# Hybrid mLSTM and sparse-attention block on one core: the output product in two passes, keys ahead of queries, masks on GpSimd

## The chip, the core and the metric

The kernel runs on one core of one Trainium2 chip. The metric is the device time of one execution in microseconds (us). The engines are TensorE (PE in the profile), VectorE (DVE), ScalarE (ACT), GpSimd (POOL) and the queues that issue DMAs, of which SyncE's (SP) issues nearly all loads. Each engine works through its own instructions in the order in which the program gives them.

## The reference, cut to what matters

512 tokens of width 1024, in float32. One combined projection feeds two head groups, whose results go through one output product.

```python
u = rmsnorm(h, norm_in[i])
proj = u @ w_in[i]                      # 1024 -> 6736 columns, split into 13 parts
...
hm = mlstm_chunkwise(mq, mk, m_v, log_i, log_f)          # 4 heads, 1024 features
hm = sigmoid(m_o) * (hm * rsqrt(mean(hm * hm)) * m_norm) * silu(m_z)
ha = dsa_attention(a_q, a_k, a_v, ix_q, ix_k, ix_w, rel_bias)   # 8 heads of 64, top 128 keys
ha = ha * silu(a_z)                                      # 512 features
h = h + concatenate([hm, ha], axis=-1) @ w_out[i]        # 1536 -> 1024
h = h + (p[i] @ w_ple[i]) * sigmoid(h @ w_ple_gate[i])
return rmsnorm(h, norm_final)
```

In the attention, logits of keys that the indexer did not select are masked, and a bias by distance is added.

## The kernel before, in words

**Products.** Every float32 operand of a product is kept as two parts, a rounded one (H) and the rest (L), and a product is three matmuls (H·H, H·L, L·H) of 128x128 weights over 512 columns. One such triple is a *step* of a dense generator: `dense_fm` (features on partitions) or `dense_tm` (tokens on partitions). Each ends with an evacuation of its PSUM bank. Dense products rotate over four PSUM banks (`mm_bank`), everything else over four others (`x_bank`).

**Weights.** `plan` lists the weight slabs in the order of use. SP loads a slab into `raw` (three buffers), ScalarE makes `wh`, VectorE or, for every second slab from 40 to 60, GpSimd makes `wl` (line 161, `work`). One job of this kind is issued per step.

**Order.** PE, VectorE, ScalarE and GpSimd are ordered by hand: `tick()` runs after each step; `later(n, f)` issues `f` after n ticks; `back` holds generators that are advanced by a credit. `weave(main, fill, rate)` gives `rate` steps of dense work to each unit of the main generator.

**Stages.** Input norm and the indexer's queries; mLSTM features; from about 240 us on the woven stages. `weave(mlstm(), ...)` takes 3.5 dense steps a unit, and its dense work ends with `attention_in(0)` (queries and keys of head pair 0, two banks `aqk`) and the attention's values (`av`, four banks). `weave(attention(), ...)` then has 32 units, (head, block of 128 queries), and 5 more to drain: `logits` (line 793) multiplies, `least` (line 803, VectorE) adds the mask and takes the smallest, ScalarE exponentiates, `norm` scales, `flip` (line 829, `pt_ps`) transposes on PE, `values` multiplies with the values, `close` gates a head pair and splits it into mixH/mixL 8 to 11. `masks` (lines 785 to 791) prepares mask plus bias of the next unit one tick after a unit: `sel[i]` plus the bias `tz`, the far part on GpSimd, the near 256 columns on VectorE. Its dense work: pairs 1 to 3 (16 steps each), `az` (the gate, four banks, 32 steps), and the first 40 of 48 steps of `project(0)`, the output product's left 512 columns over all 12 feature tiles (0 to 7 from the mLSTM, 8 to 11 from the attention). Then its last 8 steps, `project(1)` with 48, the transposes of h, the product with p, the gate product and the last norm.

`evac_aqk` (line 764) is what empties the two `aqk` banks of a pair: bank b=0 are the queries, b=1 the keys. The query part needs two ScalarE and two VectorE instructions, the key part four and four. Between the ends of the two banks lie 4 steps, because a slab of a pair holds 4 feature tiles:

```python
if b == 0:    # queries: ScalarE at ticks 0, 1; VectorE at ticks 2, 3
else:         # keys: ScalarE at ticks 0 to 3; VectorE at ticks 4 to 7
```

`evac_out` (line 887) adds the residual, which was loaded as `xr` (1 MB each) into the buffer of the bias `tz`. At the end of the program token block 3 is done in two halves (`evac_last`, line 1013), while block 2 goes through `evac_gate1` (line 1006).

Of the kernel before, what the change touches and what calls it, by code (L numbers as in the profile page):

```python
# [13 lines left out]
F32 = mybir.dt.float32  # L14
# [18 lines left out]
NTMP, NHM, NKEEP = 7, 3, 37  # L33
COST_SC, COST_CV, COST_TK, COST_MX, RATE_M, RATE_A = 1.2, 1.6, 2.0, 2.0, 3.5, 3.2
SPLITP = range(40, 62, 2)
# [13 lines left out]
def block_kernel(ctx: ExitStack, tc: tile.TileContext, x, p, w_in, b_gate, conv_w, w_out, norm_in,  # L49
# [36 lines left out]
    def f(ap):  # L86
        return ap.bitcast(F32)
# [42 lines left out]
    def slab(src, k0, nk, cols):  # L130
        plan.append(([src[k0 * P:(k0 + nk) * P, c:c + m] for c, m in cols], nk))
# [76 lines left out]
    def pair(b):  # L208
        return [(C_AQ + P * b, P), (C_AK + P * b, P)]

    for cols in ([(C_IQ, S)], [(C_MQ, S)], [(C_MK, S)], [(C_MV, S)], [(C_MV + S, S)], [(C_MO, S)], [(C_MZ, S)],
                 [(C_MO + S, S)], [(C_MZ + S, S)], pair(0), [(C_AV, S)], pair(1), pair(2), pair(3), [(C_AZ, S)]):
        nk = KP * S // sum(m for _, m in cols)
        for k0 in range(0, KT, nk):
            slab(w_in[0], k0, nk, cols)
    for c in range(2):
        for k0 in range(0, 12, KP):
            slab(w_out[0], k0, KP, [(c * S, S)])
    for c in range(2):
# [544 lines left out]
    def evac_aqk(pair):  # L764
        def go(b, ps):
            half = [slice(0, 64), slice(64, 128)]
            for s in range(2):
                h, me, other = 2 * pair + s, half[s], half[1 - s]
                if b == 0:
                    t = aq[h] = keep(f"aq{h}", F32R)  # L770
                    later(s, A.activation, t[me, :], ps[me, :], AF.Copy, 0.0, -DH ** -0.5)
                    later(s + 2, V.scalar_tensor_tensor, t[other, :], ps[me, :], -DH ** -0.5, f(t[me, :]),
                          OP.mult, OP.subtract)
                else:
                    t1, t2 = ak1[h], ak2[h] = keep(f"ak1_{h}", F32R), keep(f"ak2_{h}", F32R)
                    for q, o in enumerate((me, other)):
                        later(2 * s + q, A.activation, t1[o, :], ps[me, :], AF.Copy)
                        later(2 * s + q + 4, V.tensor_tensor, t2[o, :], ps[me, :], f(t1[me, :]), OP.subtract)
        return go

    def attention():
# [3 lines left out]
        def masks(h, i):  # L785
            n = (i + 1) * P
            t = prob[h, i] = tmp("pr", shape=(P, n))
            if i > 1:
                G.tensor_scalar(t[:, 0:n - 256], sel[i][:, 0:n - 256], tz[:, h, 0:1], None, op0=OP.add)
            if i > 0:  # L790
                V.tensor_tensor(t[:, n - 256:], sel[i][:, n - 256:], tz[:, h, :], OP.add)

# [71 lines left out]
        for k in range(NT * AH + 5):  # L864
            if k < n:
                logits(*units[k])
            if k + 1 < n:
                later(1, masks, *units[k + 1])
            if k in values_at:
                h = values_at[k]  # L870
                values(h)
                if h % 2:
                    later(4 if h > 3 else 48 if h == 1 else 24, close, h // 2)
            if k in turns_at:
                flip(*turns_at[k])
            yield
# [4 lines left out]

    hs, xr = {}, {}

    def evac_out(c):
        def ev(i, ps):
            t = hs[i, c] = keep(f"h{i}_{c}")
            V.tensor_tensor(t, ps, xr[c][:, i, :], OP.add)
            if c:
                later(2, turn_h, c, i, mm_bank("hT_ps").rearrange("p (k t) -> p k t", t=P))
        return ev  # L890

    def project(c):
        yield from dense_tm(lambda kt, i: mixH[kt][:, i * P:(i + 1) * P], lambda kt, i: mixL[kt][:, i * P:(i + 1) * P],
                            list(range(12)), evac_out(c), name="wo", late=c == 0)

    def load_residual(c):
        t = xr[c] = sp.tile([P, NT, S], F32, tag="tz", bufs=1, name=f"xr{c}")
        nc.sync.dma_start(t, x[0, :, c * S:(c + 1) * S].rearrange("(i p) c -> p i c", p=P))

# [14 lines left out]
    while not ended[0]:  # L914
        tick()
    pace[0] = 1.0
    out0 = project(0)
    weave(attention(), chain(attention_in(1), attention_in(2), attention_in(3), dense_fm(4, evac_az, name="az"),
                             (next(out0) for _ in range(40))), lambda k: RATE_A)
    load_residual(0)  # L920
    plt = sp.tile([P, SW], F32, tag="sH", bufs=1, name="plt")
    pl = plt[:, 0:NT * DPLE].rearrange("p (i c) -> p i c", c=DPLE)
    nc.sync.dma_start(pl, p[0, 0].rearrange("(i p) c -> p i c", p=P))
    run(out0)

# [12 lines left out]
    def turns():  # L938
        for i in range(NT):
            turn_h(0, i, x_bank("hT_ps", (P, 4, P)))  # L940
            yield 4.0
        for k in range(2):
# [5 lines left out]
            later(2, V.tensor_tensor, pL[k], ps, f(pH[k]), OP.subtract)  # L948
            yield 4.0

# [12 lines left out]

    load_residual(1)
    back.append(turns())
    run(project(1))


# [36 lines left out]

    def evac_gate1(i, ps):
        sg = soft(i, 1, ps, 0, S)
        later(1, add, sg, i, 1, 0, S)
        later(3, square, sg, i, 1, 0, S, fs[i][:, 1:2])
        later(4, factor, i)  # L1010
        later(6, store, i)

# [53 lines left out]
    for kt in range(KT):  # L1066
        gate_step(2, ps, slice(0, S), kt)
    evac_gate1(2, ps)
    parts = [mm_bank(f"wg3_{q}") for q in range(2)]
# [44 lines left out]
```

## Time and profile before

| what | value |
|---|---|
| median of 3 runs | 527.8 us (526.2 to 528.93) |
| the profiled execution's own time | 527.67 us |
| its span, first to last instruction | 525.1 us |
| mean granted clock of PE | 0.986 of full speed |
| ScalarE, share of the span busy | 50% |
| HBM read / written | 48.13 MB / 3.69 MB |

Times in the trace are counted from the start of the span. "Idle before, releaser" names what ended an engine's idle time. Because the matmuls' ends are modelled and overlap, the distance from one matmul's start to the next is what a matmul costs; a clean step of three is 0.70 us.

### The profile page before, as it was taken

To read this page: it belongs to the slowest core of one execution; us is meant where nothing else is said; L and a number is where in the kernel's file an instruction comes from. 1 tells how busy PE (TensorE), PEld (TensorE's weight loads), DVE (VectorE), ACT (ScalarE), POOL (GpSimd) and SP (SyncE) were. 2 spreads that over 40 slices of the span, in tenths; PEclk is the share of its full clock that TensorE was granted. 3 is DMA by queue.
4 is the path that set the end of the run, shared out by engine and by line. 5 is a ranking of instruction groups with operands and counts; after the bars stand their busy time and mean duration, and the time that the engine had idled before them with its cause. 6 is when DMAs were issued, how large, how long until landed. Compare 5 with 4: busy or idle time off the path is not lost.

```text
span 525.1 us, 6781 instructions
## 1 busy us (share of the span) xinstructions
PE 500.9 (95%) x2370; PEld 410.3 (78%) x2370; DVE 353.8 (67%) x766; ACT 265.1 (50%) x574; POOL 77.4 (15%) x118
## 2 busy tenths in 40 slices
PE   5899999999999999999979999879999999999994
PEld 4887888888788878888768888668888888778783
DVE  1944577878899599878872787785795343350944
ACT  6643676543425135654743686775775334140542
POOL 4400000000010002020221333223332110000000
PEclk9999999999999999999979999999999999999998
DMA  8442564223543133331322222121214444050213
GB/s 267 129 157 53 69 126 116 88 93 103 167 149 104 57 97 114 97 118 54 112 59 80 62 60 81 40 81 41 81 51 151 163 158 160 24 172 5 81 40 119
DMA packets 37280, 52.24 MB, mean 99 GB/s; under 512 B 4156, under 2 KB 16732, under 8 KB 37248
## 3 DMA queue, kind: packets, MB, share of 16 engines
q1 hardware_dynamic: 32192, 45.49, 27.1%
q10 hardware_dynamic: 4960, 6.31, 5.6%
q8 instruction: 18, 0.29, 0.2%
q14 instruction: 14, 0.11, 0.1%
q0 software_dynamic: 96, 0.02, 0.0%
HBM read 48.13 MB, written 3.69 MB: 99 GB/s over the span
## 4 chain that ended last, share of the span: by engine, by line
PE 76%; DVE 12%; ACT 5%; issue 3%; DMA 1%; POOL 1%; SPq 0%; POOLq 0%; ACTq 0%; DVEq 0%
PE wo L258 4%; PE wo L260 4%; PE wo L259 4%; PE mv L260 3%; PE mv L259 3%; PE mv L258 3%; PE o L238 2%; PE o L236 2%; PE o L237 2%; PE z L236 2%; PE z L238 2%; PE z L237 2%; DVE wl L161 2%; DVE ak L194 2%; PE mq L236 1%
## 5 line engine op out<-in xcount | busy, mean ns | idle before, releaser
L161 ACT ACTIVATE wh<-raw 128x512 fp32r<-128x512 f32 x140 | 83.4, 623 | 14.7 <-DMA raw<-in_w_ple_gate_dram 5.7
L161 DVE TENSOR_TENSOR wl<-raw,wh 128x512 fp32r<-128x512 f32 x118 | 78.6, 684 | 5.1 <-ACT wh L161 4.9
L161 POOL TENSOR_TENSOR wl<-raw,wh 128x512 fp32r<-128x512 f32 x22 | 29.2, 1336 | 91.2 <-issue 57.2
L258 PE MATMUL wo<-wh,mixH 128*128 128x512 f32 x96 | 39.3, 410 | 0.0
L260 PE MATMUL wo<-wh,mixL 128*128 128x512 f32 x96 | 37.8, 394 | 0.0
L259 PE MATMUL wo<-wl,mixH 128*128 128x512 f32 x96 | 37.8, 394 | 0.0
L811 ACT ACTIVATE pr<-pr,sm 128x128 f32<-128x128 f32 (+3 forms) x32 | 17.9, 560 | 17.0 <-DVE sm L803 16.8
L569 DVE MAX8 m<-sc 128x8 f32<-128x256 f32 (+2 forms) x48 | 26.4, 551 | 0.0
L236 PE MATMUL aqk<-uH,wh 128*128 128x512 f32 x64 | 26.4, 413 | 0.0
L571 DVE MATCH_REPLACE8 sc<-m,sc 128x256 f32<-128x256 f32 (+2 forms) x48 | 26.0, 541 | 0.0
L238 PE MATMUL aqk<-uH,wl 128*128 128x512 f32 x64 | 25.4, 397 | 0.5 <-DVE wl L161 0.5
L236 PE MATMUL o<-uH,wh 128*128 128x512 f32 x64 | 25.9, 404 | 0.0
L236 PE MATMUL z<-uH,wh 128*128 128x512 f32 x64 | 25.8, 403 | 0.0
L238 PE MATMUL o<-uH,wl 128*128 128x512 f32 x64 | 25.5, 399 | 0.1
L260 PE MATMUL mv<-wh,uL 128*128 128x512 f32 x64 | 25.5, 399 | 0.0
L237 PE MATMUL z<-uL,wh 128*128 128x512 f32 x64 | 25.3, 396 | 0.0
L238 PE MATMUL z<-uH,wl 128*128 128x512 f32 x64 | 25.3, 396 | 0.0
L237 PE MATMUL o<-uL,wh 128*128 128x512 f32 x64 | 25.3, 395 | 0.0
L237 PE MATMUL aqk<-uL,wh 128*128 128x512 f32 x64 | 25.3, 395 | 0.0
L259 PE MATMUL mv<-wl,uH 128*128 128x512 f32 x64 | 25.2, 394 | 0.0
L258 PE MATMUL mv<-wh,uH 128*128 128x512 f32 x64 | 25.1, 392 | 0.0
L671 POOL TENSOR_SCALAR_AFFINE_SELECT e<-e 128x128 f32<-128x128 f32 x16 | 6.8, 426 | 119.4 <-DMA e<-adram 116.4
(250 smaller groups left out, 1368.0 us busy)
## 6 DMA issues: line engine op xcount, KB each, us to landing
raw<-in_w_in_dram SPq DMA_DIRECT2D x44, 512.0 KB, 3.4
raw<-in_w_out_dram SPq DMA_DIRECT2D x12, 512.0 KB, 3.5
raw<-in_w_in_dram SPq DMA_DIRECT2D x16, 256.0 KB, 3.0
raw<-in_w_ple_gate_dram SPq DMA_DIRECT2D x8, 512.0 KB, 3.6
x<-in_x_dram SPq DMA_DIRECT2D x8, 256.0 KB, 4.4
xr<-in_x_dram SPq DMA_DIRECT2D x2, 1024.0 KB, 4.9
tdram<-tv ACTq DMA_DIRECT2D x1, 1536.0 KB
tz<-tdram ACTq DMA_DIRECT2D x1, 1024.0 KB
```

Source lines behind the costliest of these rows:

```text
L161: fn(*args)
L194: fn(*args)
L236: T.matmul(banks[b][:, 0:nt], h[:, k, bs], uH[:, kt, tok0:], start=(kt == 0), stop=False)
L237: T.matmul(banks[b][:, 0:nt], h[:, k, bs], uL[:, kt, tok0:], start=False, stop=False)
L238: T.matmul(banks[b][:, 0:nt], l[:, k, bs], uH[:, kt, tok0:], start=False, stop=(kt == KT - 1))
L258: T.matmul(banks[i], aH(kt, i), h[:, k, :], start=first, stop=False)
L259: T.matmul(banks[i], aH(kt, i), l[:, k, :], start=False, stop=False)
L260: T.matmul(banks[i], aL(kt, i), h[:, k, :], start=False, stop=last)
L569: V.max(out=m8, in_=sel[i])
L571: V.match_replace(out=sel[i], in_to_replace=m8, in_values=sel[i], imm_value=-3e38)
L671: G.affine_select(out=e[:, 0:P], in_=e[:, 0:P], compare_op=OP.is_ge, fill=-BIG, base=0, pattern=[[1, P]], channel_multiplier=-1)
L811: later(2, lambda: A.activation(t, t, AF.Exp, bias=sm[:, 0:1], scale=-1.0, accum_out=sm[:, 1:2]))
```

## The change: what it does

- **Two passes.** `project(c)` becomes `project(c, half)`: first feature tiles 0 to 7 for both column halves (32 steps each), inside the attention's weave; after it tiles 8 to 11 for both halves (16 steps each). The slabs of `w_out` are planned in that order. Each half is evacuated twice, 16 evacuations in place of 8.
- **h begins as x.** Eight loads of 256 KB bring x into the tiles `hs`, 96 and 124 ticks into the attention, in place of two loads of 1 MB after it. Evacuations add into these tiles.
- **Rate.** The attention takes 3.9 dense steps a unit (144 in all) in place of 3.2 (118). `close` of pairs 0 and 1 comes 8 and 10 ticks sooner after its `values`. `turns` transposes h every 2 ticks, not 4.
- **Keys first.** In a pair, bank b=0 are the keys (VectorE at ticks 3 to 6 after their end), b=1 the queries (ticks 2 and 3).
- **Masks.** The near part of the mask is added on GpSimd.
- **End.** Block 2's add, square, factor and store come at ticks 2, 5, 7, 13 in place of 1, 3, 4, 6.

```diff
-COST_SC, COST_CV, COST_TK, COST_MX, RATE_M, RATE_A = 1.2, 1.6, 2.0, 2.0, 3.5, 3.2
+COST_SC, COST_CV, COST_TK, COST_MX, RATE_M, RATE_A = 1.2, 1.6, 2.0, 2.0, 3.5, 3.9
...
     def pair(b):
-        return [(C_AQ + P * b, P), (C_AK + P * b, P)]
+        return [(C_AK + P * b, P), (C_AQ + P * b, P)]
...
-    for c in range(2):
-        for k0 in range(0, 12, KP):
-            slab(w_out[0], k0, KP, [(c * S, S)])
+    for half in (range(0, 8, KP), range(8, 12, KP)):
+        for c in range(2):
+            for k0 in half:
+                slab(w_out[0], k0, KP, [(c * S, S)])
...
-                if b == 0:
+                if b == 1:
                     t = aq[h] = keep(f"aq{h}", F32R)
                     later(s, A.activation, t[me, :], ps[me, :], AF.Copy, 0.0, -DH ** -0.5)
                     later(s + 2, V.scalar_tensor_tensor, t[other, :], ps[me, :], -DH ** -0.5, f(t[me, :]),
...
-                        later(2 * s + q, A.activation, t1[o, :], ps[me, :], AF.Copy)
-                        later(2 * s + q + 4, V.tensor_tensor, t2[o, :], ps[me, :], f(t1[me, :]), OP.subtract)
+                        later(s + q, A.activation, t1[o, :], ps[me, :], AF.Copy)
+                        later(2 * s + q + 3, V.tensor_tensor, t2[o, :], ps[me, :], f(t1[me, :]), OP.subtract)
...
             if i > 0:
-                V.tensor_tensor(t[:, n - 256:], sel[i][:, n - 256:], tz[:, h, :], OP.add)
+                G.tensor_tensor(t[:, n - 256:], sel[i][:, n - 256:], tz[:, h, :], OP.add)
...
-                    later(4 if h > 3 else 48 if h == 1 else 24, close, h // 2)
+                    later(4 if h > 3 else 40 if h == 1 else 14, close, h // 2)
...
-    hs, xr = {}, {}
-
-    def evac_out(c):
+    hs = {}
+
+    def load_residual(c):
+
+        for i in range(NT):
+            hs[i, c] = keep(f"h{i}_{c}")
+            nc.sync.dma_start(hs[i, c], x[0, i * P:(i + 1) * P, c * S:(c + 1) * S])
+
+    def evac_out(c, half):
         def ev(i, ps):
-            t = hs[i, c] = keep(f"h{i}_{c}")
-            V.tensor_tensor(t, ps, xr[c][:, i, :], OP.add)
-            if c:
+            V.tensor_tensor(hs[i, c], ps, hs[i, c], OP.add)
+            if half and c:
                 later(2, turn_h, c, i, mm_bank("hT_ps").rearrange("p (k t) -> p k t", t=P))
         return ev
 
-    def project(c):
+    def project(c, half):
+
         yield from dense_tm(lambda kt, i: mixH[kt][:, i * P:(i + 1) * P], lambda kt, i: mixL[kt][:, i * P:(i + 1) * P],
-                            list(range(12)), evac_out(c), name="wo", late=c == 0)
-
-    def load_residual(c):
-        t = xr[c] = sp.tile([P, NT, S], F32, tag="tz", bufs=1, name=f"xr{c}")
-        nc.sync.dma_start(t, x[0, :, c * S:(c + 1) * S].rearrange("(i p) c -> p i c", p=P))
+                            list(range(8, 12) if half else range(8)), evac_out(c, half), name="wo", late=half and c == 0)
...
-    out0 = project(0)
+    later(96, load_residual, 0)
+    later(124, load_residual, 1)
     weave(attention(), chain(attention_in(1), attention_in(2), attention_in(3), dense_fm(4, evac_az, name="az"),
-                             (next(out0) for _ in range(40))), lambda k: RATE_A)
-    load_residual(0)
+                             project(0, 0), project(1, 0)), lambda k: RATE_A)
...
-    run(out0)
+    run(project(0, 1))
...
             turn_h(0, i, x_bank("hT_ps", (P, 4, P)))
-            yield 4.0
+            yield 2.0
...
-            yield 4.0
+            yield 2.0
...
-    load_residual(1)
     back.append(turns())
-    run(project(1))
+    run(project(1, 1))
...
-    def evac_gate1(i, ps):
+    def evac_gate1(i, ps, at=(1, 3, 4, 6)):
         sg = soft(i, 1, ps, 0, S)
-        later(1, add, sg, i, 1, 0, S)
-        later(3, square, sg, i, 1, 0, S, fs[i][:, 1:2])
-        later(4, factor, i)
-        later(6, store, i)
+        later(at[0], add, sg, i, 1, 0, S)
+        later(at[1], square, sg, i, 1, 0, S, fs[i][:, 1:2])
+        later(at[2], factor, i)
+        later(at[3], store, i)
...
-    evac_gate1(2, ps)
+    evac_gate1(2, ps, (2, 5, 7, 13))
```

VectorE around the end of pair 0, in the mLSTM's weave, before (`aqk_2365` is the keys' bank, `ak_0` and `ak_1` the keys of heads 0 and 1, `st` and `go` the mLSTM's output, `e` and `sL` its scores, `wl` a weight's rest):

```order
L723 SCALAR_TENSOR_TENSOR go_1946<-hp_ps,vcols,go_1946 128x128
L723 SCALAR_TENSOR_TENSOR go_1964<-hp_ps,vcols,go_1964 128x128
L711 SCALAR_TENSOR_TENSOR st<-st,gcol 128x1
L723 SCALAR_TENSOR_TENSOR go_1946<-hp_ps,vcols,go_1946 128x128
L723 SCALAR_TENSOR_TENSOR go_1964<-hp_ps,vcols,go_1964 128x128
L194 TENSOR_TENSOR ak_0_2515<-aqk_2365,ak_0_2514 64x512
L161 TENSOR_TENSOR wl<-raw,wh 128x512
L194 TENSOR_TENSOR ak_0_2515<-aqk_2365,ak_0_2514 64x512
L161 TENSOR_TENSOR wl<-raw,wh 128x512
L194 TENSOR_TENSOR ak_1_2517<-aqk_2365,ak_1_2516 64x512
L194 SCALAR_TENSOR_TENSOR e<-st_ps,e 128x512
L194 TENSOR_TENSOR ak_1_2517<-aqk_2365,ak_1_2516 64x512
```

and with the change (`aqk_2364` is now the keys' bank, `aqk_2365` the queries'):

```order
L194 TENSOR_TENSOR ak_0_2468<-aqk_2364,ak_0_2467 64x512 x2
L712 SCALAR_TENSOR_TENSOR st<-st,gcol 128x1
L724 SCALAR_TENSOR_TENSOR go_1946<-hp_ps,vcols,go_1946 128x128
L724 SCALAR_TENSOR_TENSOR go_1964<-hp_ps,vcols,go_1964 128x128
L194 TENSOR_TENSOR ak_1_2470<-aqk_2364,ak_1_2469 64x512 x2
L194 SCALAR_TENSOR_TENSOR aq_2518<-aqk_2365,aq_2518 64x512
L194 SCALAR_TENSOR_TENSOR aq_2519<-aqk_2365,aq_2519 64x512
L712 SCALAR_TENSOR_TENSOR st<-st,gcol 128x1
L724 SCALAR_TENSOR_TENSOR go_1946<-hp_ps,vcols,go_1946 128x128
L724 SCALAR_TENSOR_TENSOR go_1964<-hp_ps,vcols,go_1964 128x128
L161 TENSOR_TENSOR wl<-raw,wh 128x512 x2
L194 SCALAR_TENSOR_TENSOR e<-st_ps,e 128x512
```

The keys' four instructions stand before the second `st` and no longer among the `wl` and `e`, and the queries' two are now the last of the pair.

GpSimd at the start of the attention, before (`pr` is a unit's mask plus bias, `sc_521`, `sc_610` and `sc_723` the selections of query blocks 1 to 3):

```order
L712 TENSOR_TENSOR st<-st,neghalf 128x1
L789 TENSOR_SCALAR pr<-sc_610,tz 128x128
L789 TENSOR_SCALAR pr<-sc_723,tz 128x256
L161 TENSOR_TENSOR wl<-raw,wh 128x512 x2
L789 TENSOR_SCALAR pr<-sc_610,tz 128x128
L789 TENSOR_SCALAR pr<-sc_723,tz 128x256
L161 TENSOR_TENSOR wl<-raw,wh 128x512 x2
L789 TENSOR_SCALAR pr<-sc_610,tz 128x128
```

and with the change:

```order
L713 TENSOR_TENSOR st<-st,neghalf 128x1
L792 TENSOR_TENSOR pr<-sc_521,tz 128x256
L790 TENSOR_SCALAR pr<-sc_610,tz 128x128
L792 TENSOR_TENSOR pr<-sc_610,tz 128x256
L790 TENSOR_SCALAR pr<-sc_723,tz 128x256
L792 TENSOR_TENSOR pr<-sc_723,tz 128x256
L161 TENSOR_TENSOR wl<-raw,wh 128x512 x2
L792 TENSOR_TENSOR pr<-sc_521,tz 128x256
L790 TENSOR_SCALAR pr<-sc_610,tz 128x128
L792 TENSOR_TENSOR pr<-sc_610,tz 128x256
L790 TENSOR_SCALAR pr<-sc_723,tz 128x256
L792 TENSOR_TENSOR pr<-sc_723,tz 128x256
```

Each head has three additions of 128x256 more here, between the same pairs of `wl`.

ScalarE at the end of the program, before (`h_0_4091` is block 2's left half, `wg_0` and `wg_1` the two halves of block 3's gate):

```order
L976 ACTIVATE sgg<-wg_4688 128x512
L986 ACTIVATE sgg,fs_4377<-h_1_4354 128x512
L1001 ACTIVATE h_0_4091<-h_0_4091,fs_4377 128x512
L194 DMA out_dram<-h_0_4091 128x512
L976 ACTIVATE sgg<-wg_0_4731 128x256
L986 ACTIVATE sgg,fs_4378<-h_1_4369 128x256
L976 ACTIVATE sgg<-wg_1_4732 128x256
L1033 ACTIVATE h_0_4096<-h_0_4096,fs_4378 128x256 x2
```

and with the change (block 2's left half is now `h_0_3783`):

```order
L978 ACTIVATE sgg<-wg_4708 128x512
L988 ACTIVATE sgg,fs_4397<-h_1_4037 128x512
L978 ACTIVATE sgg<-wg_0_4751 128x256
L988 ACTIVATE sgg,fs_4398<-h_1_4039 128x256
L1003 ACTIVATE h_0_3783<-h_0_3783,fs_4397 128x512
L194 DMA out_dram<-h_0_3783 128x512
L978 ACTIVATE sgg<-wg_1_4752 128x256
L1035 ACTIVATE h_0_3785<-h_0_3785,fs_4398 128x256 x2
```

Block 2's scaling and its store's DMA have moved behind the first half of block 3.

## Rows read from the trace of the kernel before

**Rows 1.** Page, part 1, and PEclk of part 2 (40 slices, tenths of full speed).
```profile
PE 500.9 (95%) x2370; PEld 410.3 (78%) x2370; DVE 353.8 (67%) x766; ACT 265.1 (50%) x574; POOL 77.4 (15%) x118
...
PEclk9999999999999999999979999999999999999998
```

**Rows 2.** Waits of PE, whole span: total us, times, longest us.
```profile
PE av L258 <- DVE ak L194: 2.9, 1, 2.9
PE az L236 <- DVE ak L194: 2.6, 1, 2.6
PE pt_ps L829 <- DVE sm L803: 2.2, 1, 2.2
```

**Rows 3.** Windows: length, busy us (instructions) per engine, granted clock, DMA.
```profile
265.37:268.28 2.91, 0.00 (x0) 0.03 (x1) 2.79 (x5) 0.83 (x2) 0.29 (x1) 0.89 0.39 105
268.28:274.50 6.22, 6.22 (x17) 5.06 (x18) 3.54 (x8) 2.85 (x6) 1.81 (x2) 0.50 0.17 49
291.00:349.96 58.96, 56.53 (x285) 46.54 (x283) 47.57 (x122) 42.81 (x101) 20.29 (x20) 1.00 0.21 63
334.57:336.73 2.16, 0.01 (x2) 0.03 (x1) 2.05 (x7) 0.74 (x3) 0.00 (x0) 1.00 0.45 125
349.96:352.59 2.63, 0.00 (x1) 0.03 (x1) 2.57 (x6) 0.49 (x1) 0.00 (x0) 1.00 0.59 177
352.59:356.40 3.81, 3.81 (x10) 3.02 (x11) 1.65 (x7) 1.52 (x4) 1.27 (x1) 0.55 0.06 20
```

**Rows 4.** Timeline of PE in the first gap's surroundings: start us, us, what.
```profile
263.82 0.40 PE L259 MATMUL av<-wl,uH 128*128 128x512 f32 x1
264.05 0.40 PE L260 MATMUL av<-wh,uL 128*128 128x512 f32 x1
...
268.85 0.63 PE L259 MATMUL av<-wl,uH 128*128 128x512 f32 x1
269.27 0.63 PE L260 MATMUL av<-wh,uL 128*128 128x512 f32 x1
```

**Rows 5.** Timeline of VectorE, end of pair 0.
```profile
257.60 0.68 DVE L194 SCALAR_TENSOR_TENSOR aq<-aqk,aq 64x512 fp32r<-64x512 f32 x1
...
267.44 0.69 DVE L194 TENSOR_TENSOR ak<-aqk,ak 64x512 fp32r<-64x512 f32 x1
```

**Rows 6.** Timeline of VectorE, second gap.
```profile
334.66 1.40 DVE L194 TENSOR_TENSOR ak<-aqk,ak 64x512 fp32r<-64x512 f32 x2
...
336.28 0.29 DVE L803 CUSTOM_DVE_ANT_0 pr<-lg_ps,tz 128x128 f32<-128x128 f32 x1
```

**Rows 7.** Lines by form, VectorE and GpSimd, 288 to 412 us: busy us, mean ns.
```profile
L791 DVE TENSOR_TENSOR pr<-sc,tz 128x256 f32<-128x256 f32 x24 | 11.9, 498 | 0.0
...
L789 POOL TENSOR_SCALAR pr<-sc,tz 128x256 f32<-128x256 f32 x8 | 7.8, 978 | 0.0
```

**Rows 8.** Timelines of GpSimd and VectorE at one moment.
```profile
303.77 3.00 POOL L161 TENSOR_TENSOR wl<-raw,wh 128x512 fp32r<-128x512 f32 x2 [7.91 <-issue]
...
303.79 1.82 DVE L649 TENSOR_TENSOR mixL<-go,mixH 128x512 fp32r<-128x512 f32 x1
```

**Rows 9.** Waits of VectorE, 285 to 420 us.
```profile
DVE pr L803 <- POOL wl L161: 2.7, 1, 2.7
```

**Rows 10.** Timeline of VectorE, evacuation of the output product's first half.
```profile
419.70 2.78 DVE L887 TENSOR_TENSOR h<-wo,xr 128x512 f32<-128x512 f32 x4 [3.60 <-PE wo L260]
```

**Rows 11.** Timeline of ScalarE at the end of the program.
```profile
515.25 0.72 ACT L1001 ACTIVATE h<-h,fs 128x512 f32<-128x512 f32 x1 [0.91 <-POOL fs L997]
516.00 0.37 ACTq L194 DMA_DIRECT2D out_dram<-h  x1
516.42 0.39 ACT L976 ACTIVATE sgg<-wg 128x256 f32<-128x256 f32 x1 [0.45 <-ACT h L1001]
...
518.17 0.36 ACT L976 ACTIVATE sgg<-wg 128x256 f32<-128x256 f32 x1
```

**Rows 12.** Page, part 6: DMA issues, KB each, median us to landing.
```profile
x<-in_x_dram SPq DMA_DIRECT2D x8, 256.0 KB, 4.4
```

## Prediction, made before the changed kernel was run

> **What bounds the kernel now.** I read the page's shares first, then PE's waits, then windows round each wait, then the timelines there. TensorE is busy 95% of the span, at full clock nearly everywhere [rows 1], so a change that leaves its work alone can only give back idle time, time at half clock, and what follows the last matmul. The change leaves that work alone: 12 feature tiles by 2 halves by 4 token blocks of triples as before, and the same transposes. PE's waits [rows 2] after the first microseconds are three: 2.9 us before `av`, 2.2 before `pt_ps`, 2.6 before `az`. In the windows [rows 3] VectorE is busy all through each of them (2.79 of 2.91, 2.05 of 2.16, 2.57 of 2.63 us), working off the keys of a pair. After the first and the third gap the granted clock stands at 0.50 for a while, that is 1.2 GHz in place of 2.4; after the second, shorter one it stays at 1.00. Over 291 to 350 us VectorE is busy 47.57 of 58.96 us, so it is late in bursts and not over its capacity.
>
> **The first and third gap: keys first.** A product over four banks (`av`, `az`) follows a pair whose two banks it needs again at its steps 4 and 6. Before, the later bank held the keys, whose last VectorE instruction is issued at tick 7: one tick after PE needs the bank. That wait is built into the order. Now the keys end 4 ticks earlier and are issued by tick 6, that is at +2 against a need at +4; the queries, in the later bank, are issued by tick 3 against a need at 6. So 2 and 3 steps of slack, 1.4 and 2.1 us at 0.70 us a step (three times the 0.23 us between the matmuls at 263.82 and 264.05 [rows 4]). Does VectorE keep up? It took up the old order's queries at 257.60 [rows 5]. In the order of the change six pair instructions, a `sc`, two `go` and a tiny `st` stand there one after the other: at most 9 times 0.69 us [rows 5], 6.2 us, so the last query part is done by 263.8 if ScalarE's copies are there. PE stood at its need at 265.37 [rows 3]. The wait goes:
> - gap before `av`: -2.9 us;
> - half clock after it: 6.22 us [rows 3]. At half clock matmuls start 0.42 to 0.43 us apart (268.85, 269.27), at full 0.23 [rows 4], so 45% of it is lost: -2.8;
> - gap before `az`: -2.6, and 45% of 3.81 us: -1.7.
>
> A rule to weigh here: by the Trainium skill (TensorE: Matmul & The Clock Gate, Terms) the penalty of a throttled stretch is its length times one less the granted share; that would be half of both stretches, 0.5 us more gain in all. The measured distances say 45%, and the sum goes by them.
>
> **The second gap: VectorE behind in the attention.** `pt_ps` waits for a PSUM bank that `least` at 336.28 must empty, and before it stand two key parts of 1.40 us [rows 6]. Three parts of the change lighten this. The near masks leave VectorE: 24 times 0.498, 11.9 us [rows 7] in a stage of some 120 us. The rate gives the same attention 144 steps in place of 118, 26 times 0.70 or 18 us more PE time to hide in; these steps come out of what follows, so PE's sum stays. And the keys are spread from an earlier point. In 291 to 350 us VectorE's 47.6 us would become about 41.5 (half of the masks gone) with PE time some 15% longer for the same units: 61% and not 81%. I take -2.2 for the gap.
>
> **Masks on GpSimd.** No row shows this addition on GpSimd. Its neighbours are the one-input form at 978 ns for 256 columns [rows 7] and the two-input form, two of 512 columns in 3.00 us [rows 8]: between 0.75 (half of one of these) and 1.50, and I take 0.98. 24 of them are 24 us on an engine busy 20.29 of 58.96 us [rows 3], so they fit. In time: a mask is issued one tick after a unit and used one tick after the next, 3.9 steps or 2.7 us and the unit's own matmuls later. Behind two `wl` (3.00) and a far part (0.98) it can be one or two microseconds late, and VectorE waits once so already, 2.7 us [rows 9], without PE waiting. Cost: 0 if PE's slack holds; at worst the rival below.
>
> **Second evacuations and x.** 8 more of 0.69 (four take 2.78 [rows 10]): 5.6 us on VectorE, beside PE, each with 3 to 6 steps until its bank is needed: 0. The x loads land in 4.4 us [rows 12] and are issued 10 ticks before the first use (6.9 us by the steps alone, more with the attention's matmuls). They stand on SP ahead of slabs due 12 or more steps later, and take tiles freed by the logits of heads 5 and 6, by the closed pair 1 and by the masks of head 7, all issued before: 0; if one were late, VectorE and the weights behind it would stand for some 4 us.
>
> **After the attention.** The 16 steps of `project(1, 1)` now hold all transposes: 8 of h and 2 of p, each with a VectorE part of 512 columns, 4 evacuations and 4 `wl`, 18 times 0.69 or 12.4 us against 11.2 us of steps and the transposes beside them. Tight, bounds 0 to 2; I take +0.5.
>
> **End.** ScalarE takes up block 3's first half at 516.42, right behind block 2's scaling (0.72, itself waiting for GpSimd) and its DMA issue of 0.37; the second half follows at 518.17 [rows 11]. These two leave from in front of the first half and now stand in front of the second: between 0 (the second half comes no sooner) and -1.1 (both hidden while PE finishes); I take the middle, -0.5.
>
> **Sum.** -2.9 - 2.8 - 2.6 - 1.7 - 2.2 - 0.5 = -12.7. What comes back: VectorE still meets `least` and three or four key parts at the end of each of three pairs; half a key part (0.35) each, +1.0; and +0.5 above. -11.2 on the profiled execution's own 527.67 us (its span of 525.1 and 2.6 around it; the median is 527.8) gives **516.5 us**, own range 513.5 to 519.
>
> **Rivals.**
> - *VectorE stays behind.* GpSimd slows it: beside two `wl` that took 3.00 us on GpSimd, a VectorE instruction with two inputs in SBUF took 1.82 us, where others of 512 columns take 0.69 [rows 8, 5]. 1.13 us lost per 3.0 us of GpSimd, over 24 us of masks, is 9 us, most of the 11.9 saved. Then the second gap and the third with its half clock may remain in part. If all of both: 516.5 + 2.2 + 2.6 + 1.7 = 523.0. By the Trainium skill (GPSIMD Engine Reference, Engine selection and Specifications) two-input elementwise work belongs on VectorE, GpSimd being about twice as slow and sharing its SBUF interfaces; the trace agrees, with 1.50 us against 0.69 for 512 columns. Against it: the load of 61% leaves room even so. Chance 0.12.
> - *The wait moves.* The queries now come last, and what waited for keys waits for them, or the x loads stop VectorE and the slabs: the gaps remain under other names, and only the end's 0.5 is gained: 527. For it: the order still ends with two query parts. Against: 2 us of slack by the count above. Chance 0.04.
> - *Slower: masks behind `wl`.* In each head GpSimd's queue puts masks behind weights whose `wh` ScalarE has not made yet; ScalarE is itself waiting for `least`. If each of the 11 weight pairs (slabs 40 to 60) costs PE the 2.7 us of [rows 9], that is 30 us without any clock loss: 546. It decides from the point at which masks come later than the 2.7 us and more between units allow. For it: the order above. Against: the far masks already stand in that queue, and PE did not wait. Chance 0.05.
>
> **How the numbers follow.** Forecast 0.79. The range of 513 to 521 holds nearly all of it and part of the first rival. Faster by over 0.5%, which is about what a measurement here can tell from no change: forecast and first rival, 0.91; within 0.5%: the second, 0.04; slower: the third, 0.05.
>
> **What would show it.** PE's waits: none left before `av` and `az`, none over 1 us in the attention; PEclk at full in the slices near 270 and 353 us. VectorE's line of `masks` gone, GpSimd's near 1 us each. PE idle or at half clock behind `project(0, 1)`, or VectorE waiting for GpSimd for more than some 10 us in all, would make the forecast wrong.

## The result, and the profile after

The changed kernel takes 513.78 us (median of 4 runs, 512.54 to 514.25), the kernel before in the same comparison 527.28 us (4 runs, 526.2 to 528.93). The ratio is 0.9738, its 95% interval 0.9705 to 0.977: 13.5 us faster, where 11.2 were forecast. One execution of the kernel before, in the last of the comparisons below, took 1726.98 us and is left out of them. The profiled execution took 513.7 us, with a span of 511.7 and a mean granted clock of 0.995.

The page's busy times and PEclk, answering [rows 1]:

```profile
PE 494.9 (97%) x2370; PEld 407.2 (80%) x2370; DVE 348.3 (68%) x750; ACT 264.8 (52%) x574; POOL 92.6 (18%) x142
...
PEclk9999999999999999999999999999999999999998
```

TensorE has the same 2370 matmuls and loads of weights. The slice of [rows 1] that stood at 7 is a 9 now. PE's waits in the whole span (total us, times, longest us), answering [rows 2]:

```profile
PE xt L324 <- POOL ident masks.py:199: 3.8, 1, 3.8
PE xt L324 <- DMA x<-in_x_dram: 2.7, 2, 1.7
...
PE aqk L239 <- DVE wl L161: 0.5, 1, 0.5
...
PE hT_ps L936 <- DVE h L893: 0.3, 1, 0.3
PE wg L1056 <- DVE wl L161: 0.2, 1, 0.2
```

All three waits of [rows 2] are gone. Of what is left only `aqk`, `hT_ps` and `wg` lie behind the first 40 us, 1.0 us in all. Windows of the changed kernel, answering [rows 3] (length, busy us and count of PE, PEld, DVE, ACT and POOL, granted clock, DMA share, GB/s): round the need of `av`, behind it, the attention from its first `least` to the seventeenth, and round the need of `az`:

```profile
263.50:266.50 3.00, 3.00 (x16) 2.42 (x15) 2.89 (x7) 1.92 (x6) 0.79 (x3) 1.00 0.20 66
266.50:275.00 8.50, 8.50 (x43) 7.11 (x42) 7.27 (x15) 5.22 (x11) 3.77 (x5) 1.00 0.37 87
291.30:345.03 53.73, 53.73 (x264) 44.70 (x263) 38.84 (x103) 39.51 (x90) 22.98 (x26) 1.00 0.23 71
333.00:340.00 7.00, 7.00 (x37) 5.71 (x36) 6.75 (x17) 4.04 (x11) 1.50 (x2) 1.00 0.05 21
```

VectorE is as busy in the first and last window as it was in the gaps, but PE no longer stands for it. VectorE's timeline (start us, us, what) at the end of pair 0, answering [rows 5], and PE's at the two steps of `av` that need the banks, its steps 4 and 6 counted from 0, show why:

```profile
260.47 1.38 DVE L194 TENSOR_TENSOR ak<-aqk,ak 64x512 fp32r<-64x512 f32 x2 [1.56 <-ACT ak L194]
...
262.65 1.40 DVE L194 TENSOR_TENSOR ak<-aqk,ak 64x512 fp32r<-64x512 f32 x2
264.08 1.39 DVE L194 SCALAR_TENSOR_TENSOR aq<-aqk,aq 64x512 fp32r<-64x512 f32 x2
```

```profile
264.57 0.39 PE L259 MATMUL av<-wh,uH 128*128 128x512 f32 x1
...
266.19 0.39 PE L259 MATMUL av<-wh,uH 128*128 128x512 f32 x1
```

The keys end at 264.05 and their bank is needed at 264.57; the queries end at 265.47 and theirs is needed at 266.19. The slack is 0.5 and 0.7 us, where the prediction counted 1.4 and 2.1. Its 263.8 for the last query part would be 264.8 here, since this execution runs 1.0 us later from its start (its first `aqk` at 244.7 us, not 243.7). It was missed by 0.7, because its condition did not hold: VectorE stood 1.56 us for ScalarE's copies before the first key.

Lines by form of VectorE and GpSimd, answering [rows 7] (busy us, mean ns, idle before). The `mixL` row is of the stretch 290 to 345 us alone, the other VectorE rows are of the whole span:

```profile
L893 DVE TENSOR_TENSOR h<-wo,h 128x512 f32<-128x512 f32 x16 | 11.0, 690 | 17.1 <-PE wo L261 17.0
L161 DVE TENSOR_TENSOR wl<-raw,wh 128x512 fp32r<-128x512 f32 x118 | 78.7, 685 | 5.1 <-ACT wh L161 4.8
...
L650 DVE TENSOR_TENSOR mixL<-go,mixH 128x512 fp32r<-128x512 f32 x2 | 1.4, 690 | 0.4 <-ACT mixH L648 0.4
```

```profile
L792 POOL TENSOR_TENSOR pr<-sc,tz 128x256 f32<-128x256 f32 x24 | 18.2, 759 | 0.0
L790 POOL TENSOR_SCALAR pr<-sc,tz 128x256 f32<-128x256 f32 x8 | 7.4, 922 | 0.0
```

A mask on GpSimd takes 0.76 us, against 0.50 on VectorE [rows 7]. The 16 evacuations are there, 0.69 each.

ScalarE at the end of the program, answering [rows 11]:

```profile
501.74 0.38 ACT L978 ACTIVATE sgg<-wg 128x256 f32<-128x256 f32 x1
503.06 0.42 ACT L988 ACTIVATE sgg<-h 128x256 f32<-128x256 f32 x1 [0.95 <-DVE h L985]
...
503.48 0.71 ACT L1003 ACTIVATE h<-h,fs 128x512 f32<-128x512 f32 x1
504.22 0.34 ACTq L194 DMA_DIRECT2D out_dram<-h  x1
504.61 0.38 ACT L978 ACTIVATE sgg<-wg 128x256 f32<-128x256 f32 x1 [0.42 <-PE wg L1057]
```

Block 3's second half now waits for PE's last matmul, 0.42 us; in [rows 11] it followed ScalarE's own work.

**Where the 13.5 us came from.** Marks on PE split a span into its start, the stage from the first `aqk` matmul to the first `ple` matmul, the products from there to the last matmul (57.1 or 57.2 us in every kernel), and the end from that matmul's start:

| kernel | first `aqk` | first `ple` | stage | end |
|---|---|---|---|---|
| before | 243.7 | 459.8 | 216.1 | 8.1 |
| changed | 244.7 | 447.1 | 202.4 | 7.4 |

The stage gave 13.7, the end 0.7; the start took 1.0 more, of which PE's wait for the first x loads is 1.1 (2.7 and 1.6 us). That wait was anything from 1.4 to 2.6 us in the executions below. The same marks are given for each experiment, since they hold the start apart.

### The profile page after: what moved, and what is told of

The parts are those of the page before. It is cut to its first block, busy times and chain, and to the rows that moved or that the text cites. A ratio compares the mean times of both kernels' runs of the same rounds, so it can differ in the third digit from the quotient of the medians.

```text
span 511.7 us, 6817 instructions
## 1 busy us (share of the span) xinstructions
PE 494.9 (97%) x2370; PEld 407.2 (80%) x2370; DVE 348.3 (68%) x750; ACT 264.8 (52%) x574; POOL 92.6 (18%) x142
## 4 chain that ended last, share of the span: by engine, by line
PE 87%; DVE 7%; issue 2%; ACT 1%; DMA 1%; SPq 0%; POOLq 0%; POOL 0%; ACTq 0%
PE wo L259 4%; PE wo L260 4%; PE wo L261 4%; PE mv L261 3%; PE mv L260 3%; PE mv L259 3%; PE aqk L239 3%; PE o L239 3%; PE o L237 3%; PE aqk L237 3%; PE aqk L238 3%; PE o L238 2%; PE z L237 2%; PE z L239 2%; PE z L238 2%
```

## The experiments

Theory A is the account of the prediction. Each run is compared with the kernel before on the same chip; its medians there were 527.7, 528.1 and 527.96 us for the three sets (19, 15 and 6 runs).

**Keys first alone** (e1_before_keys), in the kernel before:

```diff
-        return [(C_AQ + P * b, P), (C_AK + P * b, P)]
+        return [(C_AK + P * b, P), (C_AQ + P * b, P)]
...
-                if b == 0:
+                if b == 1:
...
-                        later(2 * s + q, A.activation, t1[o, :], ps[me, :], AF.Copy)
-                        later(2 * s + q + 4, V.tensor_tensor, t2[o, :], ps[me, :], f(t1[me, :]), OP.subtract)
+                        later(s + q, A.activation, t1[o, :], ps[me, :], AF.Copy)
+                        later(2 * s + q + 3, V.tensor_tensor, t2[o, :], ps[me, :], f(t1[me, :]), OP.subtract)
```

> The kernel before, with keys first alone (bank order and the ticks of their copies), everything else as before. Theory A (the first and third gap are built into the bank order, the second is VectorE's load in the attention): the gaps before av and az go with their half clock, 2.9 + 2.8 + 2.6 + 1.7 = 10.0 us, so 517.3 us of 527.3; a wait before pt_ps of up to 2 us stays. Theory B (VectorE's load in the attention makes the second and the third gap): only the gap before av goes with its half clock, 5.7 us, so 521.6.

Measured: 517.36 us (516.89 to 518.62), ratio 0.9813 [0.978, 0.9847], as A said. Stage 205.4 us, end 8.1. PE's waits in the attention are now:

```profile
PE av_ps L841 <- DVE sL L194: 1.8, 2, 1.1
...
PE pt_ps L829 <- DVE sm L803: 0.6, 1, 0.6
```

The waits for `av` and `az` are gone, the clock is at 0.996, and the second gap has become three small ones, 2.4 us in all. This part gives 10.7 of the stage's 13.7 us.

**The order without the ticks** (e9_before_order): only the first two pieces of that edit.

```diff
-        return [(C_AQ + P * b, P), (C_AK + P * b, P)]
+        return [(C_AK + P * b, P), (C_AQ + P * b, P)]
...
-                if b == 0:
+                if b == 1:
```

> The kernel before, with only the order of the two banks of a pair turned (keys in the earlier bank, queries in the later); the ticks of their ScalarE and VectorE instructions stay as they were. Theory A, the order is what removes the two gaps: the keys' last VectorE instruction is then issued 3 steps after the pair's end and its bank is needed at the 4th, so neither av nor az waits over 0.5 us, and the time is that of the kernel before with keys first and the new ticks, 517.4 us, within 1. Rival D, the earlier ticks are needed too: one step of slack is 0.7 us, and VectorE with four key parts of 0.7 us and other work between them overruns it; then waits of 1 to 2 us stay before av and az, and the time is 519.5 to 521.5 us. If the half clock comes back with such waits, more than that.

Measured: 519.37 us (518.77 to 519.8), ratio 0.9834 [0.9803, 0.9865]: by its time the rival's, and A's 517.4 missed by 2.0. The trace says something else. PE's waits, and a window before any of the changed code:

```profile
PE av L258 <- DVE ak L194: 0.6, 1, 0.6
...
PE az L236 <- DVE ak L194: 0.3, 1, 0.3
```

```profile
16.00:20.00 4.00, 3.89 (x13) 3.67 (x13) 3.84 (x6) 1.61 (x3) 1.88 (x3) 0.57 0.56 142
```

The two waits that the rival put at 1 to 2 us are 0.6 and 0.3 (A allowed 0.5), and the stage is 205.9 us, 0.5 longer than with the new ticks. So the order gives 10.3 of the 10.7 us and the earlier ticks the rest. Of the 2.3 us between the two spans 1.5 lie at the start (first `aqk` at 245.1, not 243.6): 3.9 us of PE time at 16 to 20 us run at a clock of 0.57, with 13 matmuls, where the kernel before has 21 at 1.00 in the same window. A clock of 0.57 over 4 us is 3.4 us at the half, and 45% of that is 1.5. No instruction there was changed, and the profiled executions of e4 and e10 have it too; why the clock was low in these isn't settled.

**All but keys first** (e3_after_nokeys): the changed kernel with e1's edit turned back.

```diff
-        return [(C_AK + P * b, P), (C_AQ + P * b, P)]
+        return [(C_AQ + P * b, P), (C_AK + P * b, P)]
```

> The changed kernel, with queries first again (bank order and ticks as before). Theory A: the gaps before av and az are back with their half clock, 10.0 us: 523.8 us of 513.8; the one before az may be some tenths shorter, since VectorE has less to do there. Theory B: only the gap before av is back, 5.7 us: 519.5.

Measured: 525.02 us (10 runs, 521.94 to 527.17), ratio 0.9949 [0.9919, 0.9979]; stage 211.6, end 7.4. A's 523.8 is nearer than B's 519.5, which lies below every run. PE's waits, and the windows behind the two gaps:

```profile
PE az L237 <- DVE ak L194: 4.4, 1, 4.4
...
PE av L259 <- DVE ak L194: 2.9, 1, 2.9
```

```profile
268.64:275.00 6.36, 6.36 (x31) 5.32 (x32) 4.83 (x10) 3.59 (x8) 3.06 (x3) 1.00 0.18 52
345.69:349.50 3.81, 3.81 (x10) 3.05 (x11) 1.64 (x5) 1.90 (x5) 1.97 (x2) 0.56 0.29 110
```

The gap before `az`, which A expected some tenths shorter, grew from 2.6 to 4.4 us at the faster rate. From the start of the pair's last matmul PE reached its stop after 7.4 us before (342.54 to 349.96) and after 6.0 here (335.29 to 341.30), while VectorE ended the last key part after 9.9 and 10.3. Before, a set of `av_ps` matmuls of 1.3 us lay between the same six steps of `az`; at the faster rate none did, so PE came to its need 1.4 us sooner. And behind the same 2.9 us before `av` as in [rows 2] the clock held: 31 matmuls in 6.36 us, where [rows 3] has 17 in 6.22.

**One gap brought back** (e10_after_pair0): the changed kernel with pair 0 alone in the old order and ticks, to price that gap and its clock.

```diff
-        return [(C_AK + P * b, P), (C_AQ + P * b, P)]
+        return [(C_AK + P * b, P), (C_AQ + P * b, P)] if b else [(C_AQ, P), (C_AK, P)]
...
-                if b == 1:
+                if b == (1 if pair else 0):
```

> The changed kernel, with pair 0 alone as before (queries in the earlier bank, keys in the later, old ticks), so that only the gap before av comes back, about 2.9 us. Theory A, the half clock behind such a gap differs from one execution to the next (0 to 7 us of it in the traces so far, of which 45% is lost): the time is 513.8 + 2.9 = 516.7 us where the clock holds and up to 519.8 where it doesn't, and the runs spread over 2 us or more. Rival E, the stretch of the first profile is the rule: 513.8 + 2.9 + 2.8 = 519.5 us, with a spread of 1 us or so.

Measured: 518.35 us (516.38, 517.56, 519.14 and 520.05, with clocks of 0.995, 0.992, 0.989 and 0.987), ratio 0.9811 [0.977, 0.9851]: A's spread, and A's range but for 0.3 us at either end. The profiled execution is the slowest of the four. PE's timeline round its one gap, and the window behind it:

```profile
266.40 0.40 PE L261 MATMUL av<-wh,uL 128*128 128x512 f32 x1
269.70 0.77 PE L259 MATMUL av<-wh,uH 128*128 128x512 f32 x1 [2.91 <-DVE ak L194]
```

```profile
269.70:276.00 6.30, 6.30 (x17) 5.19 (x18) 3.63 (x8) 2.90 (x6) 1.85 (x2) 0.52 0.20 52
```

Its stage is 208.3, so 5.9 over the changed kernel's. From start to start the gap costs 3.1 (3.30 less the usual 0.23), and 0.52 over 6.30 us is 6.0 us at the half, of which 45% is 2.7: 5.8. The run at 516.38 left no trace; by its mean clock, the changed kernel's, it has the gap with hardly any clock loss, 2.6 us over the changed kernel.

**Masks alone** (e2_before_masks), in the kernel before, and **all but the masks** (e4_after_nomasks), the same line turned back in the changed kernel:

```diff
-                V.tensor_tensor(t[:, n - 256:], sel[i][:, n - 256:], tz[:, h, :], OP.add)
+                G.tensor_tensor(t[:, n - 256:], sel[i][:, n - 256:], tz[:, h, :], OP.add)
```

> The kernel before, with the near masks on GpSimd alone. Theory A: the gaps before av and az stay with their half clock, only the wait before pt_ps goes, 2.2 us: 525.1 us of 527.3. Theory B: the second and the third gap go, 2.2 + 2.6 + 1.7 = 6.5 us: 520.8. If GpSimd slows VectorE by as much as it takes off it: 527.3.

> The changed kernel, with the near masks on VectorE again. Theory A: the rate has given VectorE enough room by itself, so no gap comes back: 513.8 us, at most 514.5. Theory B: the masks are what took the second gap away: 516 (2.2 us more).

Measured for the masks alone: 525.85 us (10 runs, 523.81 to 529.46), ratio 0.9979 [0.9949, 1.0008]. The time is near A's, and A's reason for it is wrong. PE's waits of that kernel:

```profile
PE av L258 <- DVE ak L194: 2.9, 1, 2.9
...
PE az L236 <- DVE ak L194: 2.4, 1, 2.4
PE pt_ps L829 <- DVE sm L803: 2.2, 1, 2.2
```

The second gap stands unchanged with the masks gone from VectorE. The timeline of the kernel before says why (between the second and the third row stand the two key parts and the `least` of [rows 6]):

```profile
331.88 0.70 DVE L161 TENSOR_TENSOR wl<-raw,wh 128x512 fp32r<-128x512 f32 x1
...
333.94 0.69 DVE L161 TENSOR_TENSOR wl<-raw,wh 128x512 fp32r<-128x512 f32 x1
...
336.50 0.42 DVE L791 TENSOR_TENSOR pr<-sc,tz 128x256 f32<-128x256 f32 x1
```

What stands in front of that `least` from 331.35 us on is key parts, two `wl`, another `least` and two small instructions, and no mask: the nearest ones are at 327.58, before VectorE last stood idle, and at 336.50, behind it. The stage of e2 is 213.6 us, 2.5 shorter than before; 1.4 of it is a shorter half clock behind the same first gap (see the last section) and 0.2 the third gap. All but the masks: 514.92 us (514.18 to 515.97), ratio 0.9765 [0.9731, 0.9799], 1.1 over the changed kernel and just above A's 513.8 to 514.5; stage 203.8. No `pt_ps` wait there either, but one that neither theory named:

```profile
PE az L237 <- DVE ak L194: 1.2, 1, 1.2
```

With the masks on VectorE the keys of pair 3 come 1.2 us late for `az`. That is what the masks buy once the rest is in: 1.4 us of the stage.

**Passes and rate, without keys and masks** (e5_after_passes_alone): the changed kernel with the edits of e3 and e4.

```diff
+        return [(C_AQ + P * b, P), (C_AK + P * b, P)]
...
+                V.tensor_tensor(t[:, n - 256:], sel[i][:, n - 256:], tz[:, h, :], OP.add)
```

> The two passes, x in h and the rate of 3.9 alone: the changed kernel with queries first again and the near masks on VectorE again. Theory A (the bank order makes the gaps before av and az; the second gap goes by the rate or by the keys, not by the masks): the two gaps with their half clock as where only the queries went first again, 525.0 us, and no wait before pt_ps of over 0.5 us. Theory B (the masks are needed against the second gap): 2.2 us more, 527.2, with a wait before pt_ps.

Measured: 525.98 us (10 runs, 524.62 to 528.57), ratio 0.9959 [0.994, 0.9978]; by it 524.9 to 526.9, which reaches A's 525.0 and not 527.2. The median lies midway, so the waits have to tell. Stage 215.2, end 7.4. The `pt_ps` wait is gone, so neither masks nor keys were needed against it, but `az` waits longer again:

```profile
PE az L237 <- DVE ak L194: 4.7, 1, 4.7
```

What the second gap gave back, the third took: 4.7 in place of 2.6 us.

**Keys and masks without the passes** (e6_before_keys_masks), the edits of e1 and e2 together in the kernel before, and **the old rate** (e7_after_rate32) in the changed kernel:

```diff
-COST_SC, COST_CV, COST_TK, COST_MX, RATE_M, RATE_A = 1.2, 1.6, 2.0, 2.0, 3.5, 3.9
+COST_SC, COST_CV, COST_TK, COST_MX, RATE_M, RATE_A = 1.2, 1.6, 2.0, 2.0, 3.5, 3.2
```

> The kernel before with keys first and masks on GpSimd, without the two passes and the rate. Theory A: the 2.6 us of small waits (av_ps, pt_ps) that stood with keys first alone shrink by about 1 us, the rest needs the rate: 516.4 us. Theory C (the two passes and the rate give nothing once VectorE is lightened): 514.3, that is the changed kernel's time without the half microsecond of the end.

> The changed kernel with 3.2 dense steps a unit of the attention in place of 3.9; the 26 steps left over follow the attention. Theory A: waits before av_ps and pt_ps come back in part, 1 to 2 us: 515 to 516. Theory C: no difference, 513.8.

Measured: 516.88 us (515.94 to 518.08), ratio 0.9794 [0.9763, 0.9824], stage 204.7, end 8.1; and 515.82 us (515.48 to 516.13), ratio 0.9768 [0.9745, 0.9791], stage 204.7, end 7.5. Both as A said. The old rate shows what the new one removes:

```profile
PE av_ps L842 <- DVE sL L194: 1.1, 2, 0.8
PE pt_ps L830 <- DVE sm L804: 0.6, 1, 0.6
```

The kernel with keys and masks alone has the same two rows, 1.1 and 0.6 us, and the same stage. So the two passes and h beginning as x (with the new ticks of `close` and `turns`, which no run holds apart) move the stage by nothing, and the rate (with the passes, which give it the steps) takes out 2.3 us more.

**The old end** (e8_after_end):

```diff
-    evac_gate1(2, ps, (2, 5, 7, 13))
+    evac_gate1(2, ps)
```

> The changed kernel with block 2's add, square, factor and store at ticks 1, 3, 4, 6 as before. By the prediction's term 0.5 us more, by the two traces, in which the time from PE's last matmul to the end of the span fell by 0.7, 0.7 more: 514.3 to 514.5. If the store's place does not matter: 513.8.

Measured: 513.99 us (5 runs, 513.67 to 515.53), ratio 0.974 [0.9717, 0.9762], against the changed kernel's 0.9738: no difference that the times can tell. The traces can: stage 202.4 in both, but the end is 8.3 us and not 7.4, and the first `aqk` came at 244.1, not 244.7. ScalarE's rows are those of [rows 11] again:

```profile
501.98 0.72 ACT L1003 ACTIVATE h<-h,fs 128x512 f32<-128x512 f32 x1 [0.91 <-POOL fs L999]
502.73 0.37 ACTq L194 DMA_DIRECT2D out_dram<-h  x1
503.14 0.38 ACT L978 ACTIVATE sgg<-wg 128x256 f32<-128x256 f32 x1 [0.45 <-ACT h L1003]
...
504.89 0.36 ACT L978 ACTIVATE sgg<-wg 128x256 f32<-128x256 f32 x1
```

The old end costs 0.9 us there, and a start that was 0.6 us shorter hid most of it. All the traces side with this: with the old end that time is 8.1 to 8.5 us, with the new one 7.4 or 7.5.

Put one behind the other, by the stages of the profiled executions (each good to a few tenths, as the clock held in all of these but the kernel before): keys first 10.7, masks 0.7, the passes 0.0, the rate 2.3, sum 13.7. The split between masks and rate hangs on the order: taken out last (e4), the masks are 1.4. To that the end adds 0.7.

## Why the prediction came out as it did

**Right, with its mechanism: gaps and clock.** The steps on `av` and `az` gave 10.0 us (2.9, 2.8, 2.6 and 1.7), all from keys first. Keys first alone shortened the stage by 10.7, with both waits gone, and e10's execution paid 5.9 for the first gap and its clock, where 5.7 were counted. The count of ticks behind it held in the main, with thinner margins than counted: VectorE runs one to two steps later than its ticks. The order alone leaves one step of slack, 0.7 us, and waits of 0.6 and 0.3 (e9); the new ticks leave 0.5 and 0.7 us of the 1.4 and 2.1.

**Right in size, by luck of one execution: the half clock.** The 2.8 and 1.7 us were read from one execution of the kernel before, and the 1.7 a little high: 0.55 over 3.81 us is 3.4 us at the half, 1.5 by the 45%. Behind an equal 2.9 us gap e3's execution lost nothing and e10's runs spread by 3.7 us. The sum came out because the executions of the kernel before have a mean clock of 0.982 to 0.990, and the profiled one, with 0.986, lies in the middle. That 45% of such a stretch is lost agrees with e10's 5.9 us. By the rule of the Trainium skill (TensorE: Matmul & The Clock Gate, Terms), one half, it would be 6.1; the stages are good to a few tenths and cannot tell these apart. The distances between matmuls, 0.23 and 0.42 to 0.43 us [rows 4], say 45%.

**Right outcome, wrong part: the second gap.** Its -2.2 came as said, but of the three parts that were to lighten it the masks do nothing against it (e2): none stands in the burst that PE waits for. Keys first breaks it into three waits of 2.4 us in all (e1), and the rate takes out what the masks leave of these (e7); with the passes it also does so with queries first and the masks on VectorE (e5). What counts is which work meets at a pair's end, not VectorE's load: at 333 to 340 us VectorE is busy 6.75 of 7.00 us, and PE doesn't wait. The forecast load was off too, 61% for a stretch in which 72% was measured. Here are the same sixteen units before, from the first `least` to the seventeenth, to be set beside the changed kernel's third window above:

```profile
296.31:348.55 52.24, 49.81 (x248) 41.01 (x247) 42.64 (x113) 38.76 (x89) 14.94 (x14) 1.00 0.21 63
```

The step that failed is the stretching. Less the 2.2 us of the gap these units took 50.0 us, and with the change 53.7: 7% longer and not 15%. VectorE's work fell by 3.8 us and not by the masks' 5.8, since, among others, two key parts and a `wl` more lie in the stretch (12 and 8, not 10 and 7). It cost nothing.

**Mis-sized: what comes back.** +1.5 us were set off, 0.3 came. The +1.0 for VectorE meeting `least` and key parts at three pair ends is real at the old rate, 1.7 us of waits in e7, and 0.0 in the changed kernel: the rate, which the sum credited with the second gap alone, removes these too. The +0.5 after the attention is one wait of 0.3 us before `hT_ps`.

**The sum.** For the stage the prediction has 10.0 + 2.2 - 1.5 = 10.7 us, and 13.7 were measured. Of the 3.0 between them 0.7 is keys first (10.7, not 10.0), and the rest is that masks and rate gave 3.0 (0.7 + 2.3) where 2.2 less 1.5 was left for them. The end adds 0.2, and the start, 1.0 longer in this execution, takes away what no step foresaw: 13.4 between the spans.

**Right: second evacuations and x, at nothing.** The stage of e6 and e7 is the same, 204.7 us, without and with them. The eight loads of x land in time (page's DMA issues: KB each, median us to landing), and no engine's wait names them:

```profile
h<-in_x_dram SPq DMA_DIRECT2D x8, 256.0 KB, 4.6
```

**Right: the end and the masks' price.** -0.5 was taken for the end, between 0 and -1.1; 0.7 was measured, 0.9 by e8. 0.98 us was taken for a mask, between 0.75 and 1.50; 0.76 was measured, so half of the two-input row was the better neighbour, not the one-input form.

**The rivals.** GpSimd does slow VectorE beside a `wl`, as the first rival had it. In [rows 8] a `mixL` that began 0.02 us after a `wl` of GpSimd took 1.82 us. With the change it begins 0.09 us before that `wl` (298.18 and 298.27) and takes 0.69, but another, begun within a `wl`, takes 1.38:

```profile
271.28 1.30 POOL L161 TENSOR_TENSOR wl<-raw,wh 128x512 fp32r<-128x512 f32 x1 [1.25 <-ACT wh L161]
...
271.75 1.38 DVE L650 TENSOR_TENSOR mixL<-go,mixH 128x512 fp32r<-128x512 f32 x1 [0.49 <-ACT mixH L648]
```

What the rival had wrong is that the masks do the same. Between 245 and 420 us of the changed kernel, VectorE's instructions that lie for over half their time beside a `wl` of GpSimd are 2.8 us longer in all than the medians of their like, and those beside a mask 0.4, where the rival's rate gave 9 for the masks. PE waited for neither. VectorE waited for GpSimd nowhere between 245 and 420 us, so no mask came late behind a `wl`, and the slower case has nothing for it. That elementwise work with two inputs belongs on VectorE, as the Trainium skill has it (GPSIMD Engine Reference, Engine selection, where GpSimd is about twice as slow), holds in direction, with 1.5 times here (0.76 us against 0.50), and did not decide: GpSimd had the time, and moving the masks still gave 1.1 us by the medians of e4.

A version faster than the changed kernel did not come out of these runs: behind the first 40 us its PE waits for 1.0 us in all.

## What to carry to other kernels

Where a product takes its PSUM banks in turn, compare for each bank the tick at which its last reader is issued with the step at which the bank is needed again; the bank with the long evacuation goes first, and the swap by itself was worth 10 of 13.7 us here. A small gap on a saturated PE costs more than its length when the clock falls behind it, but that second part is a matter of the execution: price it from the mean clock of several runs, not from one trace. When several edits aim at one wait, list what stands in front of it before counting load that leaves the engine elsewhere, and test each alone: one may be idle there, and be needed for another wait that only shows once the first is gone.

## What the hardware showed that was not expected

Gaps of equal length were followed by unequal stretches at half clock. Behind 2.9 us before `av`: 6.22 us at 0.50 in the kernel before [rows 3], 6.30 at 0.52 in e10, none in e3 (1.00 over 6.36 us), and about half as much in e2 and e5. Windows behind the gap before `av` in e2 and in e5, and behind the one of 4.7 us before `az` in e5:

```profile
268.83:275.00 6.17, 6.17 (x24) 5.22 (x25) 3.98 (x8) 2.79 (x6) 1.75 (x2) 0.75 0.18 53
...
269.30:275.00 5.70, 5.70 (x20) 4.78 (x21) 3.47 (x8) 2.71 (x6) 1.29 (x1) 0.72 0.19 57
348.81:356.00 7.19, 7.19 (x20) 5.68 (x21) 2.57 (x8) 2.16 (x6) 2.51 (x2) 0.61 0.36 134
```

So e2 stood 3.1 us at the half there and the kernel before 6.2. Behind 2.6 us before `az` it was 3.81 us at 0.55 [rows 3] and behind 4.4 us in e3 3.81 us at 0.56, no longer; behind the 4.7 us in e5 it was 7.19 us at 0.61, 5.6 at the half. Behind 2.2 us before `pt_ps` it stayed at 1.00 [rows 3]. Kernels with such gaps spread accordingly, 521.9 to 527.2 us at clocks of 0.993 to 0.981 in e3, and without them 515.48 to 516.13 at 0.996 to 0.997 in e7, though 515.94 to 518.08 at 0.997 to 0.993 in e6. The same happened at the start, in e9 (0.57 over 16 to 20 us, 1.00 in the kernel before). The Trainium skill (TensorE: Matmul & The Clock Gate, What's actually happening) says of the slow stretch at a kernel's start that it differs from run to run; these runs show that of the start and of gaps in the middle alike.
